# A column-strip product for shift_m, an earlier norm of x, and modulation on ScalarE, in a two-block transformer kernel

## The chip, the core and the metric

The kernel runs on one core of one Trainium2 chip. The metric is the device time of one execution in microseconds (us), as the median of several runs. Engines are named as the profile names them: PE (TensorE, the matrix array; PEld is its loading of weights), DVE (VectorE), ACT (ScalarE), POOL (GpSimd) and SP (SyncE, which here only issues the loads of the weight stream). All arithmetic is fp32. The large products split both operands into a high and a low part of the type fp32r and take three passes of one fp32r product each; the small products take fp32 as it is, which the array runs in two passes, so the profile shows two weight loads and two matmuls for one fp32 product in the code.

## What is computed

Two transformer blocks over 256 rows of width 2048. The change touches the start of the first block and the start of its feed-forward part. Cut to that:

```python
silu_c = jax.nn.silu(c)                                  # c: (1, 2048)
mod = silu_c @ w_ada[l] + b_ada[l]                       # w_ada: 2048 x 12288
shift_m, scale_m, gate_m, shift_f, scale_f, gate_f = jnp.split(mod, 6, axis=-1)
h = modulate(rmsnorm(x, g_norm_mix[l]), shift_m, scale_m)   # h * (1 + scale) + shift
proj = h @ w_in[l]                                       # 2048 x 3904
...                                                      # attention, w_out
x = x + gate_m[:, None, :] * mix
h = modulate(rmsnorm(x, g_norm_ffn[l]), shift_f, scale_f)
f = jnp.square(jax.nn.relu(h @ w_ff1[l])) @ w_ff2[l]
```

## The kernel before, in words

**The weight stream.** `make_plan` (L1511) lists some 1,100 tiles of at most 128 x 1024 (512 KB) in the order of their use. SP loads them in that order into eight raw buffers (`load`, L151): six of the pool `wraw` and two of `wraw2`. `split_next` (L164) takes the next one: a weight tile is split on ACT (`wh`, L119) and DVE (`wl`, L120) for the three-pass products (L134 to L136); a tile of w_ada is consumed at once by `ada_part` (L201). When a tile is consumed its buffer goes to the next load; SP issues in order, so a load that waits for its buffer holds all that stand behind it.

**w_ada.** Each of the six sections comes in four quarters (0 to 3) of eight tiles. For `shift_m` PE forms the products: the weight tile itself is the stationary operand, eight blocks of 128 x 128, and one column of silu(c) is moved through each (L209, eight fp32 products of one column a tile); ACT copies the finished column out (L211). The five other sections are sums of products on DVE (L218, one 128x1024 instruction a tile). `scale_m` and `shift_m` stand alternately in the plan. In the text, s0 to s7 and h0 to h7 are the eight tiles of a quarter of scale_m and of shift_m.

**The opening.** `setup` (L321) issues the small inputs and x on ACT's own queue and lays silu(c) out as a row on all partitions (`silu_row`, L250). `block1_attention` (L447) then consumes fourteen tiles of quarter 0, with `lam` and the rope tables after the sixth; then ACT squares x (L401, eight pieces), DVE makes the reciprocal root (L530, L113 and the lines 88 to 100), `x_hat` scales a 512-column group of x (L407), PE transposes it (L140), ACT copies it out as `hh` (L539), the last two tiles are consumed, `modulate` (L418) applies scale and shift (L422, DVE), and the result is split into `Ah` and `Al`.

**The rounds.** Four rounds q = 0 to 3 go over the four 512-column groups of h. A round multiplies the group by its rows of `wi_q`, `wi_kv` and six heads of `wi_d`, sixteen tiles in all. In rounds 0 to 2 the sixteen tiles of quarter q + 1 of scale_m and shift_m are spread among the first thirteen, the transposes of the next group stand after `wi_q`, and `make_h(q + 1)` stands before the last head. A transposed group takes two banks of PSUM from the pool `ps_tr` (two banks, taken in turn); so does each product of shift_m.

**ffn1** (L827) transposes and modulates x in the same way, four groups, while its first products run; there the modulation reads PSUM directly.

Of the kernel before, what the change touches and what calls it, by code (L numbers as in the profile page):

```python
# [9 lines left out]
F32 = mybir.dt.float32  # L10
# [3 lines left out]
AF = mybir.ActivationFunctionType  # L14
OP = mybir.AluOpType
AX = mybir.AxisListType
P = 128
T = 256
# [24 lines left out]
class Kernel:  # L43
    def __init__(self, ctx, tc, a, out, offs):
# [8 lines left out]
        gap = pool("gap", 1)  # L53
        gap.tile([P, 56], F32, name="gap")
        self.sm = pool("sm", 4)
# [143 lines left out]
    def ada_part(self, e, src):  # L199

        v = self.nc.vector  # L201
        sec, k = e["sec"], e["k"]
        if e["kind"] == "ada_pe":
            if k == 0:
                self.ada_col = self.tiny("ada_col", 8)
            ps = self.trp()
            for kk in range(8):
                kt = (k % 2) * 8 + kk
                self.nc.tensor.matmul(ps[:, 0:1], lhsT=src[:, kk * P:(kk + 1) * P],  # L209
                                      rhs=self.silu_c[:, kt:kt + 1], start=kk == 0, stop=kk == 7)  # L210
            self.nc.scalar.activation(self.ada_col[:, k:k + 1], ps[:, 0:1], AF.Copy)  # L211
            if k == 7:
                self.ada_end(e, self.ada_col)
            return
        junk = self.adap.tile([P, 1024], BF16, tag="ajunk", name="ajunk", bufs=1)
        if k == 0:
            self.ada_sum = self.tiny("ada_sum", 8)
        v.scalar_tensor_tensor(junk, src, 1.0, self.silu_row[:, (k % 2) * 1024:(k % 2 + 1) * 1024],  # L218
                               op0=OP.mult, op1=OP.mult, accum_out=self.ada_sum[:, k:k + 1])
        if k == 7:  # L220
            self.ada_end(e, self.ada_sum)
# [97 lines left out]
    def setup(self):  # L319
# [18 lines left out]
        self.silu_c = self.const.tile([P, 16], F32, name="silu_c")  # L338
        nc.scalar.activation(self.silu_c, c, AF.Silu)
        self.rows(self.silu_c, self.silu_row)  # L340
        self.pos_i = pos_i

# [67 lines left out]
    def x_hat_T(self, b, xh):  # L410

        ps = self.trp()
        for i in range(2):
# [4 lines left out]
    def modulate(self, A, kt, n, src, which, h):  # L418

        for i in range(n):  # L420
            k = kt + i
            self.nc.vector.tensor_scalar(h[:, i], src[:, i], self.mod["scale_" + which][:, k:k + 1],  # L422
                                         self.mod["shift_" + which][:, k:k + 1], op0=OP.mult, op1=OP.add)
        self.split(A[:, kt:kt + n], h)
# [20 lines left out]
    def block1_attention(self):  # L445
# [56 lines left out]
        def ckv_gen():  # L502
            yield
            r = self.mean_rsqrt(ssk, 2, 256, "r_k")
            tmp = tp.tile([P, 2, 1, 64], F32, name="kr_tmp")
            for tt in range(2):
# [11 lines left out]

        for _ in range(6):
            self.split_next()  # L520
        self.lam()
        self.rope_tables(tp)
        for _ in range(8):
            self.split_next()
# [24 lines left out]
        self.ahead = 3  # L549
        make_h(0, next_x(0))  # L550
        self.split_ahead()
        for q in range(4):
            xs = self.halves_of(A, range(q * 4, q * 4 + 4))
            self.linear(xs, 512, ev_q, acc=accq, first=q == 0, last=q == 3)
            if q < 3:
                hh = next_x(q + 1)
            else:
                self.add(cq_gen())
                O = self.xp.tile([P, 16, T], F32, tag="x", name="O")
# [151 lines left out]
    def diff_head(self, h, pj, O, wp, kab):  # L711
# [54 lines left out]
        for tt in range(2):  # L766
            junk = wp.tile([P, P], F32, tag="jk", name="jk", bufs=1)
            nc.scalar.activation(junk, on[:, tt], AF.Square, accum_out=ss[:, tt:tt + 1])
# [850 lines left out]
def layout(inp):  # L1619
# [20 lines left out]
    for i, k in enumerate(("shift_m", "scale_m", "gate_m", "shift_f", "scale_f", "gate_f")):  # L1640
        if k == "shift_m":
            w = wa[:, i * D:(i + 1) * D].reshape(2, 8, P, 16, P).transpose(3, 0, 2, 1, 4)
            A["ada_" + k] = np.ascontiguousarray(w).reshape(32, P, 1024)
# [104 lines left out]
```

## Time and profile before

| | |
|---|---|
| median of 3 runs | 2762.53 us (2762.14 to 2767.86) |
| the profiled execution | 2761.06 us, span 2759.3 us |
| granted TensorE clock, mean | 0.98 |
| PE busy | 2670.3 us, 97% of the span |
| DVE, ACT, POOL busy | 62%, 45%, 3% |
| opening, up to the first product of round 0 | 53.5 us |
| rounds 0, 1 and 2 | 54.0, 51.2 and 56.8 us |
| HBM | 569 MB, mean 206 GB/s |

The profiled execution lies 1.5 us below the median. Busy time is the time in which an engine had an instruction in work; consecutive matmuls overlap, since the recorded time of one includes its way through the array, so the distance between two starts tells more than the length of one. A row of windows gives the stretch, its length, then for PE, PEld, DVE, ACT and POOL the busy time and the number of instructions, then the granted clock as a share of 2.4 GHz (0.50 is the lower level, 1.2 GHz), the mean busy share of the 16 DMA engines, and GB/s. A row of a timeline gives the start, the time it took, engine, line, operation, output and inputs with their shapes, the number of instructions merged, and in brackets the idle time before it with what ended it. A row of groups gives the line, engine, operation, tiles and shapes, the count, then busy time and mean length in ns, then idle time before it.

### The profile page before, as it was taken

Reading aid. Unit: us, or ns where it says so; the run is one execution under the profiler, and the core shown is the slowest. Engines: PE = TensorE matmul, PEld = TensorE weight load, DVE = VectorE, ACT = ScalarE, POOL = GpSimd, SP = SyncE. Lnnn points to the kernel's source line nnn. Section 1 sums busy time; section 2 is a strip of 40 time slices with the busy share of each in tenths; the row PEclk is TensorE's granted clock in tenths of the full one; section 3 lists DMA queues with packets and bytes.
Section 4 is the critical chain, followed back from the end, with each engine's and each line's share of the span. In section 5 each row is a group of like instructions: output and inputs, shape, how many; then the busy total and the mean of one; then the engine's idle time right before and its main releaser. Section 6 shows DMA issues by size and latency. Waiting matters only on the chain.

```text
span 2759.3 us, 35205 instructions
## 1 busy us (share of the span) xinstructions
PE 2670.3 (97%) x12998; PEld 2287.5 (83%) x12998; DVE 1720.3 (62%) x2812; ACT 1246.1 (45%) x1816; POOL 84.5 (3%) x151
## 2 busy tenths in 40 slices
PE   7998889799999999998999999999999999999999
PEld 6997778578888888888898998888888888888887
DVE  4567988876666655567766665555555545454555
ACT  3325555344444444445555554444454444444443
POOL 0000630000000000002000000000000000000000
PEclk6999999899999999999999999999999999999999
DMA  7874888777777755554653456666566666666664
GB/s 265 294 269 132 285 289 280 265 276 236 238 237 237 236 191 190 190 181 147 223 173 106 139 164 191 191 191 191 184 190 190 191 190 191 191 191 191 191 191 152
DMA packets 163612, 568.91 MB, mean 206 GB/s; under 512 B 18288, under 2 KB 18544, under 8 KB 162800
## 3 DMA queue, kind: packets, MB, share of 16 engines
q1 hardware_dynamic: 160992, 558.70, 62.8%
q10 hardware_dynamic: 2448, 7.97, 0.8%
q8 instruction: 102, 1.67, 0.2%
q14 instruction: 70, 0.57, 0.1%
HBM read 564.50 MB, written 2.10 MB: 205 GB/s over the span
## 4 chain that ended last, share of the span: by engine, by line
PE 51%; DVE 1%; ACT 0%; issue 0%; DVEq 0%; ACTq 0%
PE acc L134 16%; PE acc L135 16%; PE acc L136 16%; PE tr L140 1%; PE at L1171 0%; DVE wl L120 0%; PE at L1168 0%; PE tr L1175 0%; ACT wh L119 0%; DVE jk L1008 0%; PE at L1232 0%; PE at L1268 0%; PE at L1248 0%; PE at L1220 0%; PE at L1217 0%
## 5 line engine op out<-in xcount | busy, mean ns | idle before, releaser
L120 DVE TENSOR_TENSOR wl<-raw,wh 128x1024 fp32r<-128x1024 f32 (+2 forms) x926 | 1071.1, 1164 | 829.9 <-ACT wh L119 827.1
L119 ACT ACTIVATE wh<-raw 128x1024 fp32r<-128x1024 f32 (+2 forms) x926 | 929.1, 1011 | 944.5 <-PE acc L136 873.8
L134 PE MATMUL acc<-wh,Ah 128*128 128x512 f32 (+2 forms) x2232 | 846.6, 379 | 4.3 <-ACT wh L119 4.2
L135 PE MATMUL acc<-wl,Ah 128*128 128x512 f32 (+2 forms) x2232 | 835.1, 374 | 12.4 <-DVE wl L120 12.1
L136 PE MATMUL acc<-wh,Al 128*128 128x512 f32 (+2 forms) x2232 | 833.5, 373 | 0.0
L135 PEld LDWEIGHTS acc<-wl,Ah 128*128 128x128 f32 x2232 | 424.5, 190 | 75.8 <-DVE wl L120 17.0
L134 PEld LDWEIGHTS acc<-wh,Ah 128*128 128x128 f32 x2232 | 424.8, 190 | 65.2 <-ACT wh L119 5.4
L136 PEld LDWEIGHTS acc<-wh,Al 128*128 128x128 f32 x2232 | 424.1, 190 | 58.7 <-DVE Al L120 0.2
L218 DVE SCALAR_TENSOR_TENSOR ajunk<-raw,silu_row 128x1024 bf16<-128x1024 f32 x160 | 195.2, 1220 | 12.4 <-ACT silu_row L250 10.1
L134 PE MATMUL acc<-wh,midh 128*128 128x512 f32 x512 | 200.3, 391 | 0.5 <-ACT wh L119 0.3
L135 PE MATMUL acc<-wl,midh 128*128 128x512 f32 x512 | 199.5, 390 | 1.1 <-DVE wl L120 1.1
L136 PE MATMUL acc<-wh,midl 128*128 128x512 f32 x512 | 199.4, 389 | 0.0
L134 PE MATMUL acc<-wh,mid2h 128*128 128x512 f32 x352 | 137.4, 390 | 0.0
L136 PE MATMUL acc<-wh,mid2l 128*128 128x512 f32 x352 | 137.0, 389 | 0.0
L135 PE MATMUL acc<-wl,mid2h 128*128 128x512 f32 x352 | 137.0, 389 | 0.0
L135 PEld LDWEIGHTS acc<-wl,midh 128*128 128x128 f32 x512 | 96.1, 188 | 21.4 <-DVE wl L120 1.9
L134 PEld LDWEIGHTS acc<-wh,midh 128*128 128x128 f32 x512 | 96.1, 188 | 20.7 <-ACT wh L119 0.7
L136 PEld LDWEIGHTS acc<-wh,midl 128*128 128x128 f32 x512 | 96.1, 188 | 20.3 <-DVE midl L120 0.4
L136 PEld LDWEIGHTS acc<-wh,mid2l 128*128 128x128 f32 x352 | 66.1, 188 | 13.7
L135 PEld LDWEIGHTS acc<-wl,mid2h 128*128 128x128 f32 x352 | 66.1, 188 | 13.6
L134 PEld LDWEIGHTS acc<-wh,mid2h 128*128 128x128 f32 x352 | 66.1, 188 | 13.5
L209 PEld LDWEIGHTS tr<-silu_c,raw 128*128 128x128 f32 x512 | 74.7, 230 | 2.3 <-ACT hh L539 1.7
(441 smaller groups left out, 2550.1 us busy)
## 6 DMA issues: line engine op xcount, KB each, us to landing
raw<-ff SPq DMA_DIRECT2D x256, 512.0 KB, 4.2
raw<-f2g SPq DMA_DIRECT2D x88, 512.0 KB, 4.0
raw<-f2u SPq DMA_DIRECT2D x88, 512.0 KB, 3.8
raw<-f2d SPq DMA_DIRECT2D x88, 512.0 KB, 4.0
raw<-wo SPq DMA_DIRECT2D x64, 512.0 KB, 4.4
raw<-wi_d SPq DMA_DIRECT2D x64, 384.0 KB, 4.7
raw<-w_fox SPq DMA_DIRECT2D x64, 384.0 KB, 3.6
raw<-ada_scale_m SPq DMA_DIRECT2D x32, 512.0 KB, 5.6
```

What stands on the lines that cost most here:

```text
L119: self.nc.scalar.activation(dst.hi, src, AF.Copy)
L120: self.nc.vector.tensor_sub(dst.lo, src, dst.hi.bitcast(F32))
L134: mm(out, lhsT=x.hi, rhs=w.hi, start=start, stop=False)
L135: mm(out, lhsT=x.hi, rhs=w.lo, start=False, stop=False)
L136: mm(out, lhsT=x.lo, rhs=w.hi, start=False, stop=stop)
L140: self.nc.tensor.transpose(out, in_, self.ident[0:n, 0:n])
L209: self.nc.tensor.matmul(ps[:, 0:1], lhsT=src[:, kk * P:(kk + 1) * P], rhs=self.silu_c[:, kt:kt + 1], start=kk == 0, stop=kk == 7)
L218: v.scalar_tensor_tensor(junk, src, 1.0, self.silu_row[:, (k % 2) * 1024:(k % 2 + 1) * 1024], op0=OP.mult, op1=OP.mult, accum_out=self.ada ...
```

## The change

`shift_m` is turned round. The host lays its part of w_ada out anew: a tile holds four blocks of 128 rows by 256 columns. A new tile `silu_z` holds 16 groups of 32 columns, zero but for the first of each, which is a column of silu(c); it is now the stationary operand (32 columns), and the weights are moved (256 columns). The four products of a tile go to the four 32-column strips of the array (`tile_position`), so to four groups of 32 partitions of one PSUM bank, `ada_bank`, held through the rounds. Four tiles accumulate one half of a quarter (256 columns); the eighth tile ends the quarter. Then ACT copies the bank to SBUF (`row`), PE multiplies its four 128-column blocks by a column of ones, which adds the four strips and turns the row into columns, and DVE adds the bias. `ada_part` shows it. The other `ps_tr` bank, `xt_bank`, is held too: it takes the transposes of x in the rounds, both halves in turn, and the sums of the closing product.

The squares and the norm of x now stand after four tiles instead of fourteen, and `lam` and the rope tables after the first transposes. The loads keep their order on both queues. `modulate` is one ACT instruction for a 128x256 block (scale and bias per partition) where it was one of DVE, in the rounds and in ffn1. The three other edits are of memory: `kr_tmp` and the squares of the heads take buffers that exist, and an unused tile grows by 128 bytes a partition.

```diff
@@ -51,7 +51,7 @@
         self.xp = pool("xp", 1)
         self.ap_ = pool("ap", 1)
         gap = pool("gap", 1)
-        gap.tile([P, 56], F32, name="gap")
+        gap.tile([P, 88], F32, name="gap")
         self.sm = pool("sm", 4)
         self.ps_acc = pool("ps_acc", 4, space=bass.MemoryType.PSUM)
         self.ps_tr = pool("ps_tr", 2, space=bass.MemoryType.PSUM)
@@ -201,16 +201,22 @@
         v = self.nc.vector
         sec, k = e["sec"], e["k"]
         if e["kind"] == "ada_pe":
-            if k == 0:
-                self.ada_col = self.tiny("ada_col", 8)
-            ps = self.trp()
-            for kk in range(8):
-                kt = (k % 2) * 8 + kk
-                self.nc.tensor.matmul(ps[:, 0:1], lhsT=src[:, kk * P:(kk + 1) * P],
-                                      rhs=self.silu_c[:, kt:kt + 1], start=kk == 0, stop=kk == 7)
-            self.nc.scalar.activation(self.ada_col[:, k:k + 1], ps[:, 0:1], AF.Copy)
+            half, g = k // 4, k % 4
+            cols = slice(half * T, half * T + T)
+            for i in range(4):
+                self.nc.tensor.matmul(self.ada_bank[i * 32:i * 32 + 32, cols], lhsT=self.silu_z[:, g * 4 + i, :],
+                                      rhs=src[:, i * T:(i + 1) * T], start=g == 0, stop=g == 3,
+                                      tile_position=(0, i * 32))
             if k == 7:
-                self.ada_end(e, self.ada_col)
+                row = self.junkp.tile([P, 512], F32, tag="junk", name="row")
+                self.nc.scalar.activation(row, self.ada_bank, AF.Copy)
+                ps = self.xt_bank
+                for i in range(4):
+                    self.nc.tensor.matmul(ps[:, i:i + 1], lhsT=row[:, i * P:(i + 1) * P], rhs=self.ones[:, 0:1],
+                                          start=True, stop=True)
+                c = slice(e["j"] * 4, e["j"] * 4 + 4)
+                v.tensor_add(self.mod[sec][:, c], ps[:, 0:4], self.s("b_" + sec)[:, c])
+                self.done.add((sec, e["j"]))
             return
         junk = self.adap.tile([P, 1024], BF16, tag="ajunk", name="ajunk", bufs=1)
         if k == 0:
@@ -337,7 +343,11 @@
         self.silu_row = self.adap.tile([P, D], F32, name="silu_row", bufs=1)
         self.silu_c = self.const.tile([P, 16], F32, name="silu_c")
         nc.scalar.activation(self.silu_c, c, AF.Silu)
+        self.silu_z = self.raw_pools[1].tile([P, 16, 32], F32, name="silu_z", bufs=1)
+        g.memset(self.silu_z, 0.0)
+        v.tensor_copy(self.silu_z[:, :, 0], self.silu_c)
         self.rows(self.silu_c, self.silu_row)
+        self.ada_bank, self.xt_bank = self.trp(), self.trp()
         self.pos_i = pos_i
 
     def load_x(self):
@@ -409,7 +419,7 @@
 
     def x_hat_T(self, b, xh):
 
-        ps = self.trp()
+        ps = self.xt_bank if self.xt_bank is not None else self.trp()
         for i in range(2):
             for tt in range(2):
                 self.T(ps[:, i * T + tt * P:i * T + (tt + 1) * P], xh[:, tt, (b * 2 + i) * P:(b * 2 + i + 1) * P])
@@ -419,8 +429,8 @@
 
         for i in range(n):
             k = kt + i
-            self.nc.vector.tensor_scalar(h[:, i], src[:, i], self.mod["scale_" + which][:, k:k + 1],
-                                         self.mod["shift_" + which][:, k:k + 1], op0=OP.mult, op1=OP.add)
+            self.nc.scalar.activation(h[:, i], src[:, i], AF.Identity, scale=self.mod["scale_" + which][:, k:k + 1],
+                                      bias=self.mod["shift_" + which][:, k:k + 1])
         self.split(A[:, kt:kt + n], h)
 
     def new_A(self):
@@ -502,7 +512,7 @@
         def ckv_gen():
             yield
             r = self.mean_rsqrt(ssk, 2, 256, "r_k")
-            tmp = tp.tile([P, 2, 1, 64], F32, name="kr_tmp")
+            tmp = tp.tile([P, 2, 1, 64], F32, tag="rtmp", name="kr_tmp")
             for tt in range(2):
                 v.tensor_scalar(kv[:, tt, 0:256], kv[:, tt, 0:256], r[:, tt:tt + 1], None, op0=OP.mult)
                 self.rope(kv[:, tt, None, 256:320], self.cos_m[:, tt], self.sin_m[:, tt], 1, tmp)
@@ -516,11 +526,7 @@
                 self.split(ckv[:, kt], ps[:, kt * T:(kt + 1) * T], self.s("g_kv_a", kt, kt + 1))
             self.done.add("ckv")
 
-        for _ in range(6):
-            self.split_next()
-        self.lam()
-        self.rope_tables(tp)
-        for _ in range(8):
+        for _ in range(4):
             self.split_next()
         ss = self.tiny("ss8", 8, bufs=2)
         for tt in range(2):
@@ -547,7 +553,10 @@
         accq = [self.acc(), self.acc()]
         pairs = [[self.acc(), self.acc()], [self.att(), self.att()]]
         self.ahead = 3
-        make_h(0, next_x(0))
+        hh = next_x(0)
+        self.lam()
+        self.rope_tables(tp)
+        make_h(0, hh)
         self.split_ahead()
         for q in range(4):
             xs = self.halves_of(A, range(q * 4, q * 4 + 4))
@@ -555,6 +564,7 @@
             if q < 3:
                 hh = next_x(q + 1)
             else:
+                self.xt_bank = None
                 self.add(cq_gen())
                 O = self.xp.tile([P, 16, T], F32, tag="x", name="O")
             for i in range(7):
@@ -764,7 +774,7 @@
         for tt in range(2):
             nc.scalar.activation(on[:, tt], po[:, tt * P:(tt + 1) * P], AF.Copy, scale=r1[:, 2 * tt:2 * tt + 1])
         for tt in range(2):
-            junk = wp.tile([P, P], F32, tag="jk", name="jk", bufs=1)
+            junk = wp.tile([P, 512], F32, tag="junk", name="junk")[:, 0:P]
             nc.scalar.activation(junk, on[:, tt], AF.Square, accum_out=ss[:, tt:tt + 1])
         r = self.mean_rsqrt(ss, 2, 128, "r_d", True)
         yield 3
@@ -1639,7 +1649,7 @@
     wa = L("w_ada")
     for i, k in enumerate(("shift_m", "scale_m", "gate_m", "shift_f", "scale_f", "gate_f")):
         if k == "shift_m":
-            w = wa[:, i * D:(i + 1) * D].reshape(2, 8, P, 16, P).transpose(3, 0, 2, 1, 4)
+            w = wa[:, i * D:(i + 1) * D].reshape(4, 4, P, 8, T).transpose(3, 0, 2, 1, 4)
             A["ada_" + k] = np.ascontiguousarray(w).reshape(32, P, 1024)
         else:
             w = wa[:, i * D:(i + 1) * D].reshape(2, 1024, 16, P).transpose(2, 0, 3, 1)
```

Three places show how the instructions now stand.

**PE in the opening** (- before, + after). The output `tr` is `ada_bank` in L207 and `xt_bank` in L140 and L215.

```order
-L209 MATMUL tr<-silu_c,raw 128x1 x56
+L253 MATMUL tr<-ident,silu_c 128x128 x16
+L207 MATMUL tr<-raw,silu_z 32x256 x8
 L140 MATMUL tr<-ident,xh 128x128 x8
-L209 MATMUL tr<-silu_c,raw 128x1 x16
+L207 MATMUL tr<-raw,silu_z 32x256 x24
+L215 MATMUL tr<-ones,row 128x1 x4
+L207 MATMUL tr<-raw,silu_z 32x256 x4
 L134 MATMUL acc<-wh,Ah 128x512
```

The transposes of x stood behind seven tiles of shift_m and stand behind two; h2 to h7 come after them, then the closing product and the first tile of quarter 1.

**ACT in the opening**, from the copies of silu's row, before and after:

```order
L250 ACTIVATE silu_row<-tr 128x512 x4
L211 ACTIVATE ada_col<-tr 128x1 x3
L438 ACT_TABLE_LOAD
L438 ACTIVATE lam_e<-lam_s 128x2
L370 ACT_TABLE_LOAD
L370 ACTIVATE sn<-ang 128x80
L375 ACTIVATE cs<-angk 128x80
L211 ACTIVATE ada_col<-tr 128x1 x4
L401 ACTIVATE junk,ss_335<-x 128x512 x8
L539 ACTIVATE hh<-tr 128x512 x2
```

```order
L256 ACTIVATE silu_row<-tr 128x512 x4
L411 ACTIVATE junk,ss_205<-x 128x512 x8
L545 ACTIVATE hh<-tr 128x512 x2
L448 ACT_TABLE_LOAD
L448 ACTIVATE lam_e<-lam_s 128x2
L380 ACT_TABLE_LOAD
L380 ACTIVATE sn<-ang 128x80
L385 ACTIVATE cs<-angk 128x80
L212 ACTIVATE row<-tr 128x512
L432 ACTIVATE hh<-hh,shift_m,scale_m 128x256 x2
L119 ACTIVATE Ah<-hh 128x512
```

The squares of x stood behind seven copies that wait for PE and stand right behind silu's row; lam and the rope tables follow the copies of the transposes. On DVE the six tiles s2 to s7 stand behind the rope tables; before, four of them stood there and three ahead.

**PE in round 0** where quarter 1 of shift_m ends, before and after:

```order
L134 MATMUL acc<-wh,Ah 128x384
L135 MATMUL acc<-wl,Ah 128x384
L136 MATMUL acc<-wh,Al 128x384
L209 MATMUL tr<-silu_c,raw 128x1 x8
L134 MATMUL acc<-wh,Ah 128x384
```

```order
L134 MATMUL acc<-wh,Ah 128x384
L135 MATMUL acc<-wl,Ah 128x384
L136 MATMUL acc<-wh,Al 128x384
L207 MATMUL tr<-raw,silu_z 32x256 x4
L215 MATMUL tr<-ones,row 128x1 x4
L134 MATMUL acc<-wh,Ah 128x384
```

The closing product, which waits for ACT's `row`, stands between the eighth tile and the next weight product; before, nothing on PE waited there.

## Rows read from the trace of the kernel before

**Rows 1.** The page: busy time of each engine; a DMA issue's size, median us to landing.
```profile
PE 2670.3 (97%) x12998; PEld 2287.5 (83%) x12998; DVE 1720.3 (62%) x2812; ACT 1246.1 (45%) x1816; POOL 84.5 (3%) x151
...
raw<-ff SPq DMA_DIRECT2D x256, 512.0 KB, 4.2
```

**Rows 2.** Windows of the opening: busy us of each engine, granted clock, DMA share, GB/s.
```profile
10.00:20.00 10.00, 9.46 (x72) 9.41 (x71) 4.08 (x10) 2.39 (x8) 0.00 (x0) 0.87 1.02 408
20.00:30.00 10.00, 10.00 (x48) 10.00 (x49) 7.71 (x30) 3.49 (x8) 0.00 (x0) 0.50 0.95 368
...
40.00:50.00 10.00, 7.16 (x33) 6.80 (x33) 5.71 (x26) 1.60 (x4) 0.00 (x0) 0.50 0.19 54
```

**Rows 3.** Timeline of the opening: start, us, engine, line, operation, tiles [idle <- releaser].
```profile
12.81 0.60 ACT L250 ACTIVATE silu_row<-tr 128x512 f32<-128x512 f32 x1 [0.35 <-PE tr L247]
...
16.78 16.59 PE L209 MATMUL tr<-silu_c,raw 128*128 128x1 f32 x80 [0.54 <-DMA raw<-ada_shift_m]
...
19.94 1.28 ACT L438 ACT_TABLE_LOAD   x1
...
25.73 1.22 DVE L218 SCALAR_TENSOR_TENSOR ajunk<-raw,silu_row 128x1024 bf16<-128x1024 f32 x1
...
33.47 0.62 ACT L401 ACTIVATE junk<-x 128x512 f32<-128x512 f32 x1
...
39.50 0.16 DVE L530 TENSOR_REDUCE ssx<-ss 128x2 f32<-128x8 f32 x1 [8.73 <-ACT junk L401]
...
42.22 0.88 DVE L407 TENSOR_SCALAR xh<-x,r_mix 128x512 f32<-128x512 f32 x2
...
44.94 0.60 ACT L539 ACTIVATE hh<-tr 128x512 f32<-128x512 f32 x1 [0.26 <-PE tr L140]
...
48.74 0.16 DVE L230 TENSOR_TENSOR shift_m<-shift_m,small 128x4 f32<-128x4 f32 x1
...
53.49 0.80 PE L134 MATMUL acc<-wh,Ah 128*128 128x512 f32 x1 [1.77 <-ACT wh L119]
```

**Rows 4.** Timeline of PE: one tile of shift_m at full clock.
```profile
73.96 1.84 PE L209 MATMUL tr<-silu_c,raw 128*128 128x1 f32 x16
```

**Rows 5.** Groups of PE by shape: passes of fp32 products over 512 and 256 columns.
```profile
L1171 PE MATMUL at<-kcat,nqT 96*128 96x512 f32 x32 | 15.0, 592 | 0.0
...
L1248 PE MATMUL at<-fkT,fqT 128*128 128x256 f32 x16 | 4.7, 378 | 0.0
```

**Rows 6.** Groups of ACT and DVE by shape: copies and modulations (count, busy, mean ns).
```profile
L539 ACT ACTIVATE hh<-tr 128x512 f32<-128x512 f32 x8 | 4.5, 595 | 22.3 <-PE tr L140 22.3
...
L697 ACT ACTIVATE E<-E,r 128x256 f32<-128x256 f32 x16 | 7.3, 503 | 7.4 <-DVE r L694 7.4
...
L422 DVE TENSOR_SCALAR hh<-hh,scale_m,shift_m 128x256 f32<-128x256 f32 x16 | 5.8, 408 | 0.0
```

**Rows 7.** Timeline of PE in round 0: the tile behind x's transposes.
```profile
63.10 1.95 PE L209 MATMUL tr<-silu_c,raw 128*128 128x1 f32 x16 [0.25 <-ACT hh L539]
```

**Rows 8.** Windows around the falls of the clock in the three rounds.
```profile
64.90:70.00 5.10, 5.10 (x30) 5.10 (x30) 2.10 (x3) 0.91 (x2) 0.00 (x0) 0.67 0.28 81
114.00:121.00 7.00, 6.75 (x43) 6.67 (x43) 2.10 (x3) 1.68 (x4) 0.00 (x0) 0.76 0.67 254
166.50:181.50 15.00, 14.75 (x65) 14.51 (x64) 4.77 (x7) 3.56 (x7) 0.00 (x0) 0.54 0.51 181
```

**Rows 9.** Timeline of PE where round 2 meets round 3.
```profile
215.46 0.49 PE L134 MATMUL acc<-wh,Ah 128*128 128x512 f32 x1 [0.78 <-ACT wh L119]
...
216.71 0.50 PE L135 MATMUL acc<-wl,Ah 128*128 128x512 f32 x1 [0.76 <-DVE wl L120]
```

**Rows 10.** Windows of the rounds 0, 1 and 2, whole.
```profile
53.50:107.50 54.00, 53.28 (x329) 51.10 (x329) 30.23 (x47) 22.95 (x43) 0.00 (x0) 0.92 0.77 272
107.50:158.70 51.20, 50.95 (x330) 49.68 (x330) 33.09 (x57) 15.75 (x29) 0.00 (x0) 0.97 0.80 290
158.70:215.50 56.80, 54.97 (x315) 52.62 (x314) 34.28 (x60) 15.17 (x29) 0.00 (x0) 0.88 0.74 253
```

## Prediction

> **What bounds the kernel now.** Begin with the page: PE is busy for 97% of the span [rows 1], so the change can only gain where PE waits, where its clock is low, or where it does less. The windows of the opening come next [rows 2]: from 20 us on the granted clock is 0.50, the lower level (1.2 GHz), and by 40 to 50 us the DMA engines have all but stopped (share 0.19): loads wait for buffers. The timeline tells why [rows 3]: five tiles of shift_m hold PE from 16.78 for 16.59 us; ACT, whose copies wait for them in order, reaches the squares of x only at 33.47; the norm starts at 39.50, xh at 42.22, and the first product of round 0 at 53.49. In the rounds PE is the bound: busy for 53.28 of 54.0, 50.95 of 51.2 and 54.97 of 56.8 us, with the DMA share at 0.74 to 0.80 and DVE busy for some 60% [rows 10]. A tile of shift_m there takes 1.84 us for 16 passes [rows 4]. A pass takes its streaming and its way through the array; 592 − 378 = 214 ns for 256 more columns [rows 5], so 256 columns of fp32 stream in 0.213 us and the way is 0.165. A tile of before therefore holds PE for 1.84 − 0.165 = 1.68 us.
>
> **The opening (A).** After the change ACT is free for the squares at 12.81 + 0.60 = 13.4. They take 39.50 − 33.47 = 6.0: 19.4. (x was requested first on its queue; the 5.5 MB of small inputs, x and six tiles come in by about 16 us at the 408 GB/s of [rows 2], an estimate, and the second half of x is squared from 16.4.) From the norm's start to the end of xh 39.50 to 43.10, 3.6: 23.0. From there to the second copy's end 43.10 to 45.54, 2.4, and 0.85 more, since both halves now use one bank and the second four transposes wait for the first copy (0.595 [rows 6] and 0.25 of handing over, as in [rows 7]): 26.3. From lam's table load to the first tile on DVE behind the rope tables 19.94 to 25.73, 5.8: 32.1. Then six tiles of scale_m at 1.3: 39.9, and three small steps: 40.5. PE starts h2 at about 26. Buffers tie the two: the loads of h6 and s7 stand behind a buffer that h4 frees, and that of h7 behind one that s3 frees (DVE, 34.7). With 4.2 us to landing [rows 1] h7 is there at 38.9. With a tile at its forecast price (below) h4 ends at 29.7 at full clock and at 32.9 at half; h7 ends at 40.1 or 41.7. Then the copy of the bank (1.1 with its handing over), the closing product (8 passes of 128-column weights, half a tile of before: 0.84, at half clock 1.66), and its handing over and the add (0.45): 42.5 or 44.9. From that add to the first product before, 48.90 to 53.49, 4.6; ACT's modulation is 0.50 where DVE's was 0.41 [rows 6], four in the chain, but two handovers go, so I keep 4.6. Round 0 starts at 47.1 or 49.5 instead of 53.5: 6.4 or 4.0 gained. I take **5.0**. If the strips run one after the other at half clock, a tile is 3.4 to 3.75, h7 ends at 49 and the round starts at 56.6: 3 lost.
>
> **The tiles in the rounds (B).** 24 tiles. No row shows two products in different strips. Lower bound, all four strips beside each other: two passes, 0.43 us. Upper bound, one after the other: 8 × 0.213 = 1.71, and, if the array must run empty at each change of shape, 2 × 0.165: 2.04. I take the case between: PE takes instructions in order, and the two passes of one product need the same strip, so the second pass of strip i runs beside the first of strip i + 1: 5 steps, 1.07 us, plus half of the 0.33: 1.24. That is 24 × (1.68 − 1.24) = **10.6**. Ends: 30.0 and −8.6. The Trainium skill (TensorEngine Tiling (Array Packing), Key Properties) has a rule that speaks against the change: changing the tiling mode drains the engine. By it the whole 0.33 would be charged and the sum would be 4 us less; no row here shows it.
>
> **The closing product (C).** PE waits 0.165 + 0.25 for the bank to be seen, 0.595 for the copy, 0.25 again, and works 0.84: 2.1 a round, three rounds, **−6.3**; nothing covers it, since the next weight product stands behind it in PE's order. If ACT is inside a split when the bank is ready it is up to 1 us more each: −9. Removed are 24 copies of a column on ACT; they lay beside PE, so nothing comes from them, except that ACT no longer stands still for each tile.
>
> **One bank for the transposes (D).** 0.85 more wait, less the 0.25 that the tile behind the transposes waited for a bank [rows 7]: 0.6, three times, **−1.8**.
>
> **Modulation on ACT (E).** Where round 2 meets round 3 PE stood idle for 0.78 and 0.76 us [rows 9], because DVE reached the modulation late, behind sums that wait for PE. ACT has no such sums in its queue there: **+1.5** (0 to 2). In ffn1 the same move takes 16 instructions off DVE, beside PE's work: 0, and up to 2 if DVE was late.
>
> **The clock (F).** Three falls [rows 8] lost 5.1 × 0.33 + 7 × 0.24 + 15 × 0.46 = 10.3 us. Each begins behind x's transposes and the tile after them, some 3 us with few columns moved [rows 7], and is drawn out by further tiles at half clock. The new tiles move 1,024 columns each instead of eight, so falls should be fewer; but the wait in D and the closing stretch (2.1 us) are new quiet places. I take **+4**, with ends at −6 and +10.3.
>
> **Sum.** 5.0 + 10.6 − 6.3 − 1.8 + 1.5 + 4 = 13.0. From the profiled execution's 2761.06 that is 2748.0; this execution lay 1.5 below the median of the runs, so 2748 to 2749.5; I name **2748**. Loads are no bound at this size: the rounds would be some 51 us on the mean (162.0 less 8.0, by three), the DMA share 0.81 where it is 0.77.
>
> **Rivals.**
> - *The strips run wholly beside each other.* For it: they share no column and no partition of PSUM. Against: in-order issue and the two passes. A tile is 0.43 to 0.76, say 0.6, so B is 26 and the sum 28: 2733. It ends there, not lower, because at 46 us a round the DMA share would be 0.9. The Trainium skill (TensorE: Matmul & The Clock Gate, Part 3) states that products in different strips run at once, and gives 2.38 times for three strips; by 2.38 a tile would be some 0.7 us as an estimate.
> - *The strips don't overlap, so the change does not do what it says.* For it: no row shows an overlap, and one tile moves 8 × 256 columns where 16 loads of 128 columns went before, which is the same time to 2%. Then a tile is 2.04, B is −8.6, A about −1, F 0: −1 − 8.6 − 6.3 − 1.8 + 1.5 = −16, so 2777, slower. It decides from a tile of 1.68 + 2.4/24 = 1.78 us on, with A, C, D, E and F as forecast (2.4 together).
> - *The closing stretch drops the clock in each round.* For it: falls do follow some 3 us with few columns [rows 7, 8], and the eighth tile with its closing is 3.3 us. Three falls more of 3.4 us on the mean of [rows 8], and no gain in F: 13 − 4 − 10.3 = −1.3, so 2762, no change.
>
> **Chances.** The forecast 0.45 (2740 to 2757), strips wholly beside each other 0.23, strips one after the other 0.20, clock falls 0.12. A measurement of this kernel can tell about 0.2% from no change, 5.5 us: faster is below 2757.0, slower above 2768.1. Faster: nearly all of the first case and the second, 0.65. No change: most of the clock's case and the edge of the forecast, 0.16. Slower: 0.19. The range takes in the forecast, the first rival's 2733 with a little below, and the clock's case; what it leaves out is the second rival: 2729 to 2768.
>
> **What would show it.** The distance from the first pass of L207 to the next weight product, at full clock: 1.1 to 1.4 us by the forecast, under 0.8 by the first rival, 1.7 or more by the second. The first product of round 0 at 47 to 50 us. PE idle before L215 for about 1.2 us in each quarter, before the second transposes about 0.85. No idle time at the start of round 3. The windows behind the transposes and behind L215: clock near 1.00 or 0.50. The forecast is wrong if the rounds take 53.5 us or more on the mean, or 48 or less, or if the first product of round 0 comes after 52.

## The result, and the profile after

The changed kernel takes 2717.6 us (median, 2716.0 to 2721.9) where the kernel before took 2762.4 in the same comparison: ratio 0.9836, 95% interval 0.9819 to 0.9853. That is 45 us less, where the forecast was 13 and the range ended at 2729. The direction was right and the size missed. The span of the profiled execution (first to last instruction) is 2716.2 us, 43.1 below the 2759.3 of before.

The page (busy time of each engine; answers to [rows 1]):

```profile
PE 2621.4 (97%) x12774; PEld 2219.7 (82%) x12774; DVE 1706.3 (63%) x2777; ACT 1261.0 (46%) x1820; POOL 84.7 (3%) x152
```

PE's busy share is still 97%, and it is busy for 48.9 us less. A share of busy time tells nothing of a change that takes work from the bounding engine; three landmarks do. The three stretches below hold 43.0 of the 43.1 us:

| stage | before | after | gain | forecast |
|---|---|---|---|---|
| opening, to round 0's first product | 53.5 | 47.1 | 6.4 | 5.0 |
| rounds 0 to 2 | 162.0 | 135.3 | 26.7 | 8.0 |
| ffn1, first to last modulation | 53.0 | 43.1 | 9.9 | 0 |

The rounds 0, 1 and 2 of the changed kernel, windows with columns as in [rows 10]:

```profile
47.10:94.30 47.20, 45.30 (x272) 37.61 (x272) 26.83 (x40) 22.92 (x38) 0.00 (x0) 0.93 0.87 320
94.30:139.40 45.10, 42.82 (x273) 35.80 (x273) 35.35 (x56) 20.84 (x30) 0.00 (x0) 1.00 0.90 333
139.40:182.40 43.00, 41.60 (x269) 35.78 (x266) 32.75 (x54) 17.73 (x25) 0.00 (x0) 1.00 0.91 330
```

The clock no longer falls in rounds 1 and 2; the 0.93 of round 0 is its first 6 us, which begin at the lower clock as before. PE in round 2, a tile of shift_m, then the last tile with the closing product (answers to [rows 4]):

```profile
166.47 0.34 PE L136 MATMUL at<-wh,Al 128*128 128x384 f32 x1
166.74 0.64 PE L207 MATMUL tr<-raw,silu_z 128*32 128x256 f32 x8
167.31 0.45 PE L134 MATMUL acc<-wh,Ah 128*128 128x384 f32 x1
167.59 0.34 PE L135 MATMUL acc<-wl,Ah 128*128 128x384 f32 x1
...
169.35 0.34 PE L136 MATMUL acc<-wh,Al 128*128 128x384 f32 x1
169.62 0.64 PE L207 MATMUL tr<-raw,silu_z 128*32 128x256 f32 x8
170.98 1.05 PE L215 MATMUL tr<-ones,row 128*128 128x1 f32 x8 [0.72 <-ACT row L212]
171.89 0.42 PE L134 MATMUL acc<-wh,Ah 128*128 128x384 f32 x1
172.15 0.34 PE L135 MATMUL acc<-wl,Ah 128*128 128x384 f32 x1
```

The neighbours of the tile of [rows 4], in the kernel before:

```profile
73.79 0.33 PE L136 MATMUL at<-wh,Al 128*128 128x384 f32 x1
...
75.66 0.42 PE L134 MATMUL at<-wh,Ah 128*128 128x384 f32 x1
75.92 0.33 PE L135 MATMUL at<-wl,Ah 128*128 128x384 f32 x1
```

From the start of a tile to the next weight product is 0.57 us: two passes of 0.213 and 0.14 besides. The neighbours are moved apart a little too: from 166.47 to 167.59 is 1.12, and two products without a tile between take 2 x 0.173, so a tile costs 0.77. The same distance around the tile of before is 2.13 (73.79 to 75.92), so that one cost 1.78.

The opening (answers to [rows 2] and [rows 3]), windows and then single rows of the timeline:

```profile
10.00:20.00 10.00, 4.64 (x37) 3.63 (x36) 2.47 (x4) 7.42 (x19) 0.00 (x0) 0.96 1.03 409
20.00:30.00 10.00, 5.72 (x40) 2.77 (x40) 5.08 (x31) 3.99 (x6) 0.00 (x0) 0.52 0.52 192
30.00:40.00 10.00, 2.16 (x16) 0.40 (x16) 9.26 (x26) 0.67 (x3) 0.00 (x0) 0.65 0.68 238
```

```profile
14.04 0.62 ACT L411 ACTIVATE junk<-x 128x512 f32<-128x512 f32 x1
...
25.30 1.12 PE L140 MATMUL tr<-ident,xh 128*128 128x128 f32 x4 [0.69 <-ACT hh L545]
...
28.60 0.16 DVE L450 TENSOR_TENSOR neglam<-lam_e 128x1 f32<-128x1 f32 x1 [4.53 <-ACT lam_e L448]
...
32.86 1.22 DVE L224 SCALAR_TENSOR_TENSOR ajunk<-raw,silu_row 128x1024 bf16<-128x1024 f32 x1
...
38.66 1.08 PE L207 MATMUL tr<-raw,silu_z 128*32 128x256 f32 x8 [3.95 <-DMA raw<-ada_shift_m]
...
40.52 1.87 PE L215 MATMUL tr<-ones,row 128*128 128x1 f32 x8 [0.78 <-ACT row L212]
...
47.08 0.79 PE L134 MATMUL acc<-wh,Ah 128*128 128x512 f32 x1 [1.01 <-ACT wh L119]
```

Three landmarks are within a microsecond of the forecast's (squares at 13.4, tiles of scale_m behind the tables at 32.1, round 0 at 47.1). The rows also show the price of the new order, which the forecast did not set against the old one. DVE waits 4.53 us for `lam`'s exponential, because ACT stands at the copies of `hh` ahead of it; six tiles of scale_m stand behind. And the DMA share is 0.52 from 20 to 30 us, where it was 0.95 before [rows 2]. SP's own waits from 14 to 48 us (total, times, longest) tell whose buffers the loads wait for:

```profile
SPq L161 <- PE tr L207: 14.4, 5, 10.9
SPq L161 <- DVE ajunk L224: 6.3, 2, 5.4
```

The longest, 10.9 us, is for a tile of shift_m, which now stands behind the transposes in PE's order; the next, 5.4, for a tile of scale_m behind the tables on DVE.

### The profile page after: what moved, and what is told of

The parts are those of the page before. It is cut to its first block, busy times and chain, and to the rows that moved or that the text cites. A ratio compares the mean times of both kernels' runs of the same rounds, so it can differ in the third digit from the quotient of the medians.

```text
span 2716.2 us, 34723 instructions
## 1 busy us (share of the span) xinstructions
PE 2621.4 (97%) x12774; PEld 2219.7 (82%) x12774; DVE 1706.3 (63%) x2777; ACT 1261.0 (46%) x1820; POOL 84.7 (3%) x152
## 4 chain that ended last, share of the span: by engine, by line
PE 52%; DVE 1%; issue 0%; ACT 0%; DVEq 0%; ACTq 0%
PE acc L134 16%; PE acc L135 16%; PE acc L136 16%; PE tr L140 1%; PE at L1181 1%; DVE wl L120 0%; PE at L1178 0%; PE tr L1185 0%; ACT wh L119 0%; DVE jk L1018 0%; PE at L1242 0%; PE at L1278 0%; PE at L1258 0%; PE at L1230 0%; PE at L1227 0%
## 5 line engine op out<-in xcount | busy, mean ns | idle before, releaser
L136 PE MATMUL acc<-wh,mid2l 128*128 128x512 f32 x352 | 137.0, 389 | 0.0
L135 PE MATMUL acc<-wl,mid2h 128*128 128x512 f32 x352 | 137.0, 389 | 0.0
L134 PEld LDWEIGHTS acc<-wh,midh 128*128 128x128 f32 x512 | 96.1, 188 | 20.7 <-ACT wh L119 0.7
L134 PEld LDWEIGHTS acc<-wh,mid2h 128*128 128x128 f32 x352 | 66.1, 188 | 13.6
L135 PE MATMUL acc<-wl,O2h 128*128 128x512 f32 (+1 forms) x208 | 72.0, 346 | 0.3 <-DVE wl L120 0.3
```

The source lines that it names most:

```text
L134: mm(out, lhsT=x.hi, rhs=w.hi, start=start, stop=False)
L135: mm(out, lhsT=x.hi, rhs=w.lo, start=False, stop=False)
L136: mm(out, lhsT=x.lo, rhs=w.hi, start=False, stop=stop)
```

## The experiments

The theory: the missing 30 us are the tiles (0.77 us instead of 1.24), the clock, whose falls are gone, and ffn1's modulation, whose move the forecast priced at nothing. The rivals: the rounds gain through the clock alone; ffn1 gains because it is reached earlier; the norm's new place is worth the opening's 6 us. All times in us; "rounds" are 0 to 2 together, the last four columns are of the profiled execution. The kernel before had medians of 2762.5 to 2764.6 beside these runs.

| run | median | ratio to before (95%) | round 0 at | rounds | ffn1 | span |
|---|---|---|---|---|---|---|
| one_strip | 2745.5 | 0.9934 (0.9920 to 0.9949) | 50.8 | 161.2 | 43.2 | 2744.7 |
| two_alt | 2727.8 | 0.9870 (0.9856 to 0.9885) | 47.5 | 143.7 | 42.8 | 2725.8 |
| two_adj | 2727.5 | 0.9870 (0.9856 to 0.9885) | 47.5 | 143.9 | 42.7 | 2726.1 |
| f_dve | 2726.4 | 0.9866 (0.9851 to 0.9881) | 47.2 | 135.4 | 52.8 | 2724.8 |
| before_f_act | 2755.3 | 0.9964 (0.9943 to 0.9986) | 55.2 | 162.0 | 43.7 | 2753.6 |
| m_dve | 2723.1 | 0.9852 (0.9838 to 0.9867) | 46.2 | 138.9 | 43.3 | 2720.7 |
| late_norm | 2712.7 | 0.9814 (0.9800 to 0.9829) | 41.5 | 134.4 | 42.9 | 2708.7 |
| tables_late | 2719.5 | 0.9844 (0.9827 to 0.9860) | 42.9 | 140.4 | 43.4 | 2716.9 |
| strips_only | 2726.8 | 0.9871 (0.9850 to 0.9892) | 41.8 | 137.0 | 52.4 | 2722.8 |
| early_only | 2757.9 | 0.9981 (0.9970 to 0.9993) | 54.3 | 155.5 | 52.3 | 2752.8 |
| late_close | 2714.1 | 0.9821 (0.9804 to 0.9838) | 47.2 | 130.7 | 43.1 | 2713.6 |
| best | 2707.8 | 0.9799 (0.9782 to 0.9815) | 41.5 | 129.7 | 43.1 | 2706.0 |

### One strip instead of four

```diff
-matmul(ada_bank[i*32:i*32+32, cols], ..., start=g == 0, stop=g == 3, tile_position=(0, i*32))
+matmul(ada_bank[0:32, cols], ..., start=g == 0 and i == 0, stop=g == 3 and i == 3, tile_position=(0, 0))
```

> The changed kernel with all four products of a tile of shift_m in the same strip (32 columns, one group of 32 partitions), everything else in its place; the closing product adds 32 rows instead of 128. Theory: the rounds gained because four strips stream at once; in one strip the eight passes of a tile follow one another, 8 x 0.213 = 1.7 us at full clock, so 24 tiles take 24 x (1.8 - 0.7) = 26 us more and the opening some 3 to 7 more: 2745 to 2752 us if the clock stays up, up to 2760 if its falls come back with the longer tiles. Rival: the rounds gained through the clock (a tile moves 1,024 columns instead of eight) and not through the strips: the three rounds stay within 5 us of the changed kernel's 135.3, and the run takes 2718 to 2725 us.

Measured: rounds of 161.2 us, 25.9 more than the changed kernel's. PE around a tile, and the three rounds:

```profile
176.80 0.34 PE L136 MATMUL at<-wh,Al 128*128 128x384 f32 x1
177.07 1.91 PE L207 MATMUL tr<-raw,silu_z 128*32 128x256 f32 x8
178.91 0.44 PE L134 MATMUL at<-wh,Ah 128*128 128x384 f32 x1
179.19 0.33 PE L135 MATMUL at<-wl,Ah 128*128 128x384 f32 x1
```

```profile
50.80:105.80 55.00, 53.03 (x273) 40.91 (x273) 27.69 (x41) 23.65 (x39) 0.00 (x0) 1.00 0.78 270
105.80:159.90 54.10, 52.74 (x273) 40.95 (x272) 35.72 (x58) 19.90 (x29) 0.00 (x0) 1.00 0.83 284
159.90:211.90 52.00, 50.64 (x266) 40.33 (x266) 31.62 (x52) 17.37 (x24) 0.00 (x0) 1.00 0.78 266
```

The tile is 1.84 us instead of 0.57. The eight passes now follow one another; in four strips they don't. The windows settle the second question: the clock is 1.00 in all three rounds although the strips don't overlap. So the falls of [rows 8] can go without the strips' overlap. These rounds are as long as before all the same: what the clock gives back, the longer tiles (from 176.80 to 179.19 is 2.39, less 0.35 is 2.04 each for 1.78, 24 x 0.26 = 6.2), the closing and the transposes (6.3, below) take. The theory holds; the rival that the clock did it alone falls.

### Two strips, in two orders

```diff
+p = (i % 2) * 32     # two_alt: strips 0, 1, 0, 1
+p = (i // 2) * 32    # two_adj: strips 0, 0, 1, 1
-matmul(ada_bank[i*32:i*32+32, cols], ..., tile_position=(0, i*32))
+matmul(ada_bank[p:p+32, cols], ..., tile_position=(0, p))
```

> The changed kernel with the four products of a tile in two strips, in the order 0, 1, 0, 1; the closing product adds 64 rows. With four strips a tile takes 0.57 us to the next product, with one 1.84, so b = (1.84 - 0.57) / 6 = 0.212 us a pass in the fullest strip and 0.15 besides. Theory: a tile lasts as long as its fullest strip, in whatever order the products stand; two strips have four passes each: 0.15 + 4 x 0.212 = 1.0 us, and the run takes 24 x 0.43 = 10 us more than the changed kernel: 2726 to 2731 us. Rival (the forecast's reading: passes start in order, and only neighbours in different strips run beside each other): the second pass of each product beside the first of the next, 5 steps and 0.15: 1.2 us, 2733 us.

> As the run before, with the order 0, 0, 1, 1. Theory (a tile lasts as long as its fullest strip, whatever the order): again 1.0 us and 2726 to 2731 us. Rival (passes start in order): only one of eight passes has a neighbour in another strip, 7 steps and 0.15: 1.63 us, 24 x 1.06 = 25 us more than the changed kernel, 2743 us.

Measured: 2727.8 and 2727.5 us, and the same tile in both. First 0, 1, 0, 1, then 0, 0, 1, 1:

```profile
160.73 1.06 PE L208 MATMUL tr<-raw,silu_z 128*32 128x256 f32 x8
161.72 0.44 PE L134 MATMUL at<-wh,Ah 128*128 128x384 f32 x1
```

```profile
160.81 1.06 PE L208 MATMUL tr<-raw,silu_z 128*32 128x256 f32 x8
161.81 0.44 PE L134 MATMUL at<-wh,Ah 128*128 128x384 f32 x1
```

0.99 and 1.00 us, as the theory had it from the other two sizes: 0.15 and 0.212 for each pass of the fullest strip (2, 4 or 8). The order of the products makes no difference. The forecast's five steps rested on the order; that reading falls.

### ffn1's modulation

```diff
 # f_dve: the changed kernel, but in modulate()
+if which == "f": self.nc.vector.tensor_scalar(h[:, i], src[:, i], scale, shift, op0=OP.mult, op1=OP.add)
 # before_f_act: the kernel before, but in modulate()
+if which == "f": self.nc.scalar.activation(h[:, i], src[:, i], AF.Identity, scale=scale, bias=shift)
```

> The changed kernel with ffn1's modulation back on DVE (the rounds' stays on ACT). Theory: of the 45 us gained, about 10 come from ffn1, where DVE no longer makes hh behind the scale tiles' sums and the wl halves. Then this run takes about 2727 us (2725 to 2730); the path up to the last product of w_out is as in the changed kernel (487.8 us), and the distance from the first to the last modulation of ffn1 goes from 43.5 back to about 53.5 us. Rival: ffn1's start gained because it is reached 34 us earlier and its loads stand differently; then 2716 to 2720 us, and the distance stays at about 43.5.

> The kernel before with one edit: ffn1's modulation on ACT. Theory: about 10 us gained, 2750 to 2754 us, all of it between the first and the last modulation of ffn1. Rival (the gain there needs the earlier start): 2759 to 2763 us, no change.

Measured: with the modulation back on DVE the stretch is 52.8 us again (2726.4); moved alone in the kernel before it is 43.7, though it is reached no earlier (2755.3, 1.3 above the range named and 9.1 below the kernel before beside it). The theory holds in both, the rival falls. One window from the first to the last modulation in each: kernel before, f_dve, before_f_act, changed kernel.

```profile
528.40:581.40 53.00, 47.70 (x209) 37.62 (x207) 45.17 (x71) 17.64 (x20) 0.00 (x0) 0.96 0.71 257
```

```profile
494.30:547.20 52.90, 48.89 (x209) 38.35 (x208) 45.17 (x72) 17.55 (x20) 0.00 (x0) 0.94 0.71 253
```

```profile
529.80:573.40 43.60, 43.28 (x195) 35.47 (x194) 37.36 (x56) 24.42 (x34) 0.00 (x0) 0.94 0.80 294
```

```profile
494.80:537.90 43.10, 42.78 (x198) 35.23 (x197) 37.26 (x56) 24.35 (x35) 0.00 (x0) 0.97 0.80 294
```

DVE loses 7.9 us of work; the stretch loses 9.9. PE has 11 instructions fewer in the shorter stretch, 198 for 209, so its length says a little more than the run gains: f_dve's whole span is 8.6 us longer than the changed kernel's. The timeline of the kernel before tells why, DVE first, then PE's waits, then DVE's waits for `Ah` in the stretch (total, times, longest):

```profile
543.83 0.99 DVE L422 TENSOR_SCALAR hh<-tr,scale_f,shift_f 128x256 f32<-128x256 f32 x2
545.51 0.69 DVE L120 TENSOR_TENSOR Al<-hh,Ah 128x512 fp32r<-128x512 f32 x1 [0.70 <-ACT Ah L119]
546.12 1.22 DVE L218 SCALAR_TENSOR_TENSOR ajunk<-raw,silu_row 128x1024 bf16<-128x1024 f32 x1
...
547.27 1.22 DVE L120 TENSOR_TENSOR wl<-raw,wh 128x1024 fp32r<-128x1024 f32 x1
```

```profile
548.54 0.50 PE L135 MATMUL at<-wl,Ah 128*128 128x512 f32 x1 [1.49 <-DVE wl L120]
553.12 0.50 PE L135 MATMUL acc<-wl,Ah 128*128 128x512 f32 x1 [1.55 <-DVE wl L120]
557.27 0.50 PE L135 MATMUL acc<-wl,Ah 128*128 128x512 f32 x1 [1.13 <-DVE wl L120]
```

```profile
DVE Al L120 <- ACT Ah L119: 5.0, 7, 0.8
```

DVE makes `hh`, then stands for 0.70 until ACT has made `Ah` from it, and everything behind, `wl` too, comes later by both. 45.17 us of work and the seven such waits in the stretch (0.78 and six of 0.70) are 50.2 of 53: DVE bounded this stretch, under a PE that looked 90% busy. After the move PE is busy for 42.78 of 43.1 us, so there is little left to gain there.

### The rounds' modulation, and the strips alone

```diff
 # m_dve: the changed kernel, but in modulate()
+if which == "m": self.nc.vector.tensor_scalar(...)
 # strips_only: both modulations on DVE, and the norm and the tables in their old place
```

> The changed kernel with the rounds' modulation back on DVE (ffn1's stays on ACT). Theory (the forecast's own term): 1.5 us longer, 0 to 3, so about 2719 us, with idle time of some 0.8 us at the start of a round where DVE comes late. Rival: the modulation on ACT is worth as much in the rounds as in ffn1, so 8 to 10 us longer, about 2726, with PE idle at each of three starts for 2 us and more.

> The strip products alone: the changed kernel with the norm of x behind fourteen tiles and the tables after the sixth as in the kernel before, and with both modulations on DVE. Theory (the parts add up: late norm 2708.7 in its profiled execution, ffn1's modulation 8.6, the rounds' 4.5): 2722 in the profiled execution, 2723 to 2727 us in the median, so some 37 of the 45 us are the strips', 12 of them in the opening, where round 0 starts at 41 to 42 us. Rival: the modulation on ACT is what lets the rounds follow the shorter tiles, and without it the clock falls or DVE holds PE: 2732 us or more.

Measured: 2723.1 and 2726.8. In m_dve the waits of [rows 9] are back to the hundredth:

```profile
185.10 0.50 PE L134 MATMUL acc<-wh,Ah 128*128 128x512 f32 x1 [0.78 <-ACT wh L119]
...
186.36 0.50 PE L135 MATMUL acc<-wl,Ah 128*128 128x512 f32 x1 [0.76 <-DVE wl L120]
```

The run is 5.5 us above the changed kernel's median and 4.5 in the spans, between the theory's 0 to 3 and the rival's 8 to 10; PE does not stand for 2 us at each start, as the rival had it. At the start of round 3 it is 2.7 behind: its opening is 0.9 shorter, its rounds 3.6 longer. PE also waits 0.72 us for `xh`, which DVE makes late, ahead of the last transposes (0.70 in the kernel before), and one window (145 to 150 us) shows a granted clock of 0.67 that the changed kernel has not. The other 1.8 us come after the start of round 3, 0.76 of them in the wait for `wl` above. strips_only came out at its expected number: 36.5 of the 43.1 us are the strips' with all that hangs on them, the closing product, the held banks and the clock (opening 11.7, rounds 25.0).

### The place of the norm and of the tables

```diff
 # late_norm: the changed kernel with
-for _ in range(4): self.split_next()
+for _ in range(6): self.split_next()
+self.lam(); self.rope_tables(tp)
+for _ in range(8): self.split_next()
 # early_only: the kernel before with the reverse edit
 # tables_late: the changed kernel with lam and the tables behind make_h(0, hh) and split_ahead()
```

> The changed kernel with the squares and the norm of x back behind fourteen tiles, and lam and the rope tables back after the sixth, as in the kernel before. Theory: the early norm brings the 6 us by which round 0 starts earlier, so round 0 starts near 53 us and the run takes 2722 to 2725 us. Rival: the five tiles of shift_m that held PE, and ACT behind it, for 16.59 us take under 1 us each with four strips, so the squares come early wherever they stand: round 0 starts at 44 to 48 us and the run takes 2714 to 2719 us.

> The kernel before with the early norm alone: the squares and the norm of x after four tiles, lam and the rope tables behind the first transposes. Theory: with tiles of shift_m that hold PE for 3.3 us at the lower clock the early norm brings what the forecast said, 4 to 6 us, round 0 starts at 47 to 50 us, 2756 to 2759 us; it costs time only where the tiles are short. Rival: it costs time with long tiles too, since lam and the tables on DVE, behind the transposes, hold up six tiles of scale_m and the loads behind them: round 0 at 53 us or later, 2762 us or more.

> The changed kernel with lam and the rope tables behind the first modulation and the first weight splits. Theory: in the changed kernel they hold DVE from 23.57 to 32.86 us, and six tiles of scale_m, and the loads that wait for their buffers, stand behind them; without them round 0 starts 5 to 8 us earlier, at 39 to 42 us, and the run takes 2709 to 2713 us. Rival: the 9 us on DVE and the table loads on ACT then stand ahead of the halves wl and wh in round 0, and PE waits there instead: 2716 to 2720 us.

Measured: late_norm 2712.7, round 0 at 41.5. The theory falls and the rival holds, by more than it said: the new place of the norm and of the tables together costs the changed kernel 5.6 us in the opening. late_norm's windows and rows:

```profile
10.00:20.00 10.00, 5.91 (x53) 3.76 (x52) 6.44 (x23) 4.75 (x7) 0.00 (x0) 0.93 1.02 408
20.00:30.00 10.00, 3.54 (x28) 0.61 (x24) 9.08 (x38) 6.02 (x18) 0.00 (x0) 0.50 1.02 410
```

```profile
17.33 0.16 DVE L450 TENSOR_TENSOR neglam<-lam_e 128x1 f32<-128x1 f32 x1 [0.27 <-ACT lam_e L448]
...
20.74 0.61 ACT L411 ACTIVATE junk<-x 128x512 f32<-128x512 f32 x1
...
21.59 1.22 DVE L224 SCALAR_TENSOR_TENSOR ajunk<-raw,silu_row 128x1024 bf16<-128x1024 f32 x1
```

Here DVE does the tables from 16.6 to 21.6, with a wait of 0.27 instead of 4.53, and the DMA share stays at 1.02 up to 30 us. ACT still reaches the squares at 20.7, since tiles of shift_m no longer stop it.

In early_only round 0 starts at 54.3, where the rival had it, so with long tiles the early norm brings nothing either. (Before had 53.5, and before_f_act, whose opening has the same code, 55.2: 0.8 later is no loss that can be told.) Its median nevertheless lies 0.19% below before, in the theory's range but not for its reason: in the profiled execution, 6.5 us below before, 6.4 are round 2 (50.4 instead of 56.8), whose fall of the clock does not occur there. This run tells nothing of the norm beyond the opening.

tables_late moved the cost: round 0 starts 4.2 us earlier, with the norm still early, so most of the 5.6 us is the tables' place; what the rest is, no run separates. Round 0 then takes 52.4 us instead of 47.3:

```profile
54.49 1.30 PE L140 MATMUL tr<-ident,xh 128*128 128x128 f32 x4 [3.49 <-DVE xh L417]
```

The second transposes' `xh` waits behind the tables on DVE, and the granted clock is 0.74 from 50 to 58 us. The rival's total holds; it had PE waiting for `wl` and `wh`, and it waits for `xh`. The tables cost where they stand, unless DVE has slack there, as early in the opening.

### Closing and transposes one tile later; both edits

```diff
 # late_close, in ada_part (k == 7): the copy of the bank stays, the four products and the add become
+self.pend.append([0, close])           # issued by get() behind the next weight tile
 # in next_x (q > 0): the second half's transposes
+self.pend.append([1, lambda: half(1)])
 # best: late_close with late_norm's edit
```

> The changed kernel with two pieces of PE's order moved in the rounds: the closing product stands one weight tile later than the copy of the bank, and the second four transposes one weight tile later than the first. Theory: PE's waits of 0.72 us for the copy and 0.69 us for hh go, three times each, 4 us in all: 2712 to 2715 us, nothing new in their place, since the modulation was ready 3 us before the next round. Rival: the modulation comes later by the moved tile (2.1 us) behind two splits on ACT, and PE waits for it at the start of the next round: 2716 to 2720 us.

> The changed kernel with the closing product and the second transposes one weight tile later, and with the norm of x and the tables where they stood before. Theory: both gains add up, 5 us from the norm's old place and 4 from the waits: 2707 to 2710 us. Rival: as in the run before, the waits only move: 2712 to 2714 us.

Measured: 2714.1 and 2707.8. PE's waits before L215 and the second transposes are gone in the rounds, and the three take 130.7 us (135.3): 4.6 less, against the 4 expected. In the profiled executions 1.2 of it is given back between 1218 and 1288 us, behind ffn1; the cause stays open. late_close's own interval overlaps the changed kernel's, so that its gain shows in the rounds but not yet in the total. `best` beats both kernels: 0.9799 of before, and its interval does not touch the changed kernel's (0.9819 to 0.9853); its round 2 takes 41.4 us.

## Why the prediction was wrong, step by step

The letters are the forecast's terms.

**B, the tiles: the main miss.** "5 steps, 1.07 us, plus half of the 0.33: 1.24" against 1.68 of before. Measured, with the effect on the neighbours: 0.77 against 1.78, so 24 x 1.01 = 24.2 instead of 10.6. The wrong step is "PE takes instructions in order, and the two passes of one product need the same strip". What counts is the number of passes of the fullest strip, in whatever order they stand (two_alt, two_adj). The first rival had the tile (0.43 to 0.76, "say 0.6") and set it at 0.23; its "for" stood on what the products share, the forecast's on an order that no row showed. The Trainium skill (TensorE: Matmul & The Clock Gate, Part 3) says that products in different strips run at once, and here the trace agrees: 1.84 us in one strip, 0.57 in four, 3.2 times. Another rule of the Trainium skill, that a change of tiling mode drains the engine (TensorEngine Tiling (Array Packing), Key Properties), would by the forecast's own size for it (2 x 0.165) charge 0.33 a tile; what a tile costs beyond its two passes is 0.77 − 0.43 = 0.34. But the tile in one strip carries the same 0.34 (2.04 − 1.70), and no run tells a drain from other handing over in it.

**E, ffn1: priced at 0, measured 9.9.** "In ffn1 the same move takes 16 instructions off DVE, beside PE's work: 0, and up to 2 if DVE was late." The step that failed is "beside PE's work": DVE's work bounded that stage, and PE waited for `wl`. The forecast shows no row of it; its window has PE at 90% and DVE at 45.17 of 53 us. By the whole run the move is worth 8.6 (f_dve). In the rounds E was forecast 1.5 and is 2.8 to the start of round 3 (178.7 in strips_only, 175.9 in late_norm); the waits of [rows 9] were read rightly, and the wait for `xh` ahead of the last transposes (0.71 in strips_only) was left out.

**F, the clock: 4, measured 6 to 9.** Granted clock times length: 12.7 us were lost in the three rounds before [rows 10], 3.3 after. By difference from the other terms (26.7 − 24.2 + 5.0 + 1.3 − 2.8) it is 6.0; the 3 us between the two stay open. The forecast's reason, more columns moved in a tile, is not shown: falls come with the turned products too (0.67 in m_dve, 0.74 in round 0 of tables_late), and in early_only a fall went without them.

**C and D held.** C, the closing: 2.80 from the last tile's predecessor (169.35) to the second product after (172.15) less 1.12 is 1.68 a round, 5.0 for 6.3. D: 0.69 less the 0.25 of [rows 7], 1.3 for 1.8. late_close took back 4.6 of the two.

**A, the opening: the number right, its cause wrong.** 47.1, at the near end of the forecast's 47.1 to 49.5. But the forecast followed one order through and never asked what short tiles do in the old order: 41.5. The 6.4 us are +11.7 for the strips, −5.6 for the new place of the norm and the tables, and 0.2 for the modulation (41.8 in strips_only, 41.5 in late_norm). So it was luck that the total fitted: two effects that the forecast did not tell apart.

**Sum.** 13.0 + 13.6 (B) + 9.9 + 1.3 (E) + 2.0 (F) + 1.3 (C) + 0.5 (D) + 1.4 (A) = 43.0, of 43.1 in the spans. Behind the forecast's 13.0 stands what each term missed; F is the remainder of the rounds, so the sum closes there by construction. The range failed because its low end was the first rival with nothing for ffn1. Of the loads the forecast said that the DMA share would limit the rounds at 46 us and 0.9; they went to 43.0 at 0.91, and to 41.4 in `best`.

## What to carry to other kernels

Before a move between engines is priced at nothing, take the window of that very stage, and add to the busy time of the engine that is relieved the waits inside its own chain: in ffn1 DVE's 45 us and its seven waits for ACT were 50 of 53 us. When a change makes a blocking step short, ask what it does in the old order first; a reordering that was meant to go around the block may then only cost. Where no row shows a price and two readings are far apart, let the range hold the whole span from one to the other together with what the other terms may add.

## What the runs showed of the hardware

- Four fp32 products (32 stationary, 256 moved columns) took 0.57 us to the next product in four column strips, 0.99 and 1.00 in two, 1.84 in one: 0.15 and 0.212 for each pass of the fullest strip. In two strips the order of issue made no difference of more than 0.01 us.
- The same rounds can lose or keep the clock: round 2 took 56.8 us in the kernel before (granted clock 0.54 for 15 us) and 50.4 in early_only (1.00 throughout), with the same code, reached 0.7 us later. What decides it, no run shows.
